# The meta tokens' state of gated linear attention in 128 rows, padded with zeros, instead of 16

## The chip, the cores and the metric

The kernel runs on one core of a Trainium2 chip. The metric is the device time of one execution in microseconds (us), lower is better. The core has five engines with a queue each: PE multiplies matrices (its weight loads have a row of their own in the profile, PEld), DVE and ACT work on vectors, POOL does small work and issues some transfers, and SP issues most of the transfers.

## The reference, cut to what matters

One decoder layer over 16 learned meta tokens followed by 512 tokens of width 1024. A retention branch and a gated linear attention branch (GLA) are computed from one input projection, gated, merged and projected. The GLA branch has four heads with keys of 128 and values of 256; its state decays by a gate of its own for every token and key channel:

```python
log_a = jax.nn.log_sigmoid((glr @ w_gate_up + b_gate)) / GLA_GATE_TAU
...
b = jnp.cumsum(ac, axis=2)
b_last = b[:, :, -1]
q_dec = qc * jnp.exp(b)
k_end = kc * jnp.exp(b_last[:, :, None] - b)
...
def step(state, xs):
    q_n, k_n, v_n, a_n = xs
    inter = jnp.einsum('bihd,bhde->bihe', q_n, state)
    state = state * jnp.exp(a_n)[..., None] + jnp.einsum('bjhd,bjhe->bhde', k_n, v_n)
    return state, inter
```

The meta tokens come first, so the state with which token 0 of the 512 starts is the sum over the 16 meta tokens of (key decayed to the end of the meta tokens) times value. Their outputs are dropped at the end.

## The kernel before, in words

Everything lies on 128 partitions ("rows" below). The 512 tokens are four blocks of 128; the meta tokens are a fifth, small block. Nearly all time goes to large projections by `quad` (a Strassen-like scheme of seven or so products; a product is 24 matmuls of line 327) and to branch products (lines 198 to 202). Every fp32 weight tile is split into a high and a low half by `split` (line 163: a copy on ACT, then a subtraction on DVE), so that each product is three matmuls of a faster type. Raw weights lie in six buffers (`wraw`), halves in three (`wsplit`); a load starts when a buffer is free.

Attention is woven in between: `weave` runs a generator of products and one of attention steps in turns. The planner of the program then gives each engine one fixed order by its own estimate of when things are ready, so instructions may stand elsewhere than the code has them. An engine works through its order without overtaking, apart from weight loads.

GLA is done for two pairs of heads, `gla_attention(0)` beside the products of `gla_g(0)`, and `gla_attention(1)` beside those of `gla_g(1)` (lines 1214 and 1217). Its steps, in the code's order (lines 1027 to 1057):

- `decays(b)`: splits the log gates `la` of block b into `lah` and `lal`, multiplies them on PE by 0/1 sums (`gsum`) into `ge` and `gf`, takes exponentials on ACT (`gX`), and makes four decayed copies of keys and queries on DVE (`gK`, `gQ`).
- `meta_state`: the same for the 16 meta tokens. Lines 976 and 977 multiply `lah` and `lal`, cut to 16 rows, by `gsm` (16 by 16); the exponential gives `gkm` (128 by 16), which is multiplied by the keys. `meta_state2` transposes it on PE (line 987, result in `gmt`) and copies it to `gkmt` on ACT (line 989), a tile of 16 rows; `meta_state3` multiplies it by the values `gvm`, also of 16 rows (line 995, a plain fp32 matmul, which the profile shows as two instructions), and DVE copies the result to `gS`, the first state (line 997).
- `scores(b)`: `gc` on PE (lines 957 to 961, the last a transpose), masked into `stb` by DVE (line 965).
- `values(b)`: lines 1006, 1007 and 1010 on PE: queries by state and scores by values into `go`, and the new state's addend `gsu`, which DVE adds (line 1012).

`gvm` is made once for each pair of heads, on ACT (lines 593 and 762). `gsm` comes from a constant through a small transfer and a cast on POOL (lines 739 to 742). Four `stb` tiles are set to zero on POOL (lines 1211 to 1213).

Of the kernel before, what the change touches and what calls it, by code (L numbers as in the profile page):

```python
# [21 lines left out]
F32 = mybir.dt.float32  # L22
F32R = mybir.dt.float32r
# [29 lines left out]
def constants():  # L53
    c = {}
    pos = np.concatenate([np.arange(NM, NM + 256), np.arange(HM),
                          np.arange(NM + 256, TT), np.arange(HM, NM)]).astype(np.float32)
    half = P
    inv = (10000.0 ** (-np.arange(half) / half)).astype(np.float32)
    ang = (pos[None, :] * inv[:, None].astype(np.float32)).astype(np.float32)
    c["rope"] = np.stack([np.cos(ang), np.sin(ang)], axis=1).astype(np.float32)  # L60

    j = np.arange(P)[:, None]
    cc = np.arange(T)[None, :]
    jm = np.arange(NM)[:, None]
    dec = np.zeros((4, P, 2, T), np.float64)
    for h in range(4):
        g = 1.0 - 2.0 ** (-5.0 - h)
        dec[h, :, 0] = np.where(cc >= j, g ** np.maximum(cc - j, 0).astype(np.float64), 0.0) / 16.0
        dm = g ** (NM + cc - jm).astype(np.float64) / 16.0
        for r in range(4):  # L70
            dec[h, 32 * r:32 * r + NM, 1] = dm
    c["decay"] = dec.astype(np.float32)

    m = np.arange(P)[:, None]
    i = np.arange(P)[None, :]
    U = (m <= i).astype(np.float64)
    mid = (np.arange(P) // 32) * 32 + 15
    Dm = U - U[:, mid]

    def level(w):  # L80
        s = (np.arange(P) // w) * w
        right = (np.arange(P) // w) % 2 == 1
        r = (m >= s[None, :]) & (m <= i)
        l = (m > i) & (m < (s + w)[None, :])
        return np.where(right[None, :], r, l).astype(np.float64)

    END = (m > i).astype(np.float64)
    c["gsum"] = (np.concatenate([U, Dm, level(64), level(32), END], axis=1) / 16.0).astype(np.float32)
    mm = np.arange(NM)
    c["gsum_meta"] = ((mm[:, None] > mm[None, :]) / 16.0).astype(np.float32)  # L90

    jj, ii = np.arange(P)[:, None], np.arange(P)[None, :]
    mA = (jj < 64) & (ii >= 64)
    mB = (jj // 64 == ii // 64) & (jj % 64 < 32) & (ii % 64 >= 32)
    mD = (jj // 32 == ii // 32) & (jj <= ii)
    c["gmask"] = np.stack([mA, mB, mD], axis=1).astype(np.int32)

    sel = np.zeros((P, P), np.float32)
    for g in range(4):
        for r in range(4):  # L100
            sel[32 * g + np.arange(NM), 32 * r + np.arange(NM)] = 1.0
    c["sel"] = sel
    oc = np.zeros((P, 1), np.float32)
    oc[[16, 48, 80]] = 1.0
    c["onecol"] = oc
    return c
# [3 lines left out]
def hybrid_kernel(ctx: ExitStack, tc: tile.TileContext, I, out: bass.AP):  # L110
# [51 lines left out]
    def split(hi, lo, src):  # L162
        return nc.scalar.copy(hi, src), nc.vector.tensor_sub(lo, src, hi.bitcast(F32))  # L163
# [10 lines left out]
    def act(ins):  # L174
        return queue("act", ins)
# [37 lines left out]
    def weave(dense, chain, skip=0):  # L213

        for n, _ in enumerate(dense):
            tick()
            if n >= skip:
                next(chain, None)
        for _ in chain:
            pass  # L220
# [298 lines left out]
    g1 = gctx.enter_context(tc.tile_pool(name="g1", bufs=1))  # L519
    la = g1.tile([P, 5, 512], F32, name="la")  # L520
    gsum = g1.tile([P, 640], F32R, name="gsum")
    gsm = g1.tile([NM, NM], F32R, name="gsm")
    gmask = g1.tile([P, 3, P], I32, name="gmask")
    gvm = [g1.tile([NM, 512], F32, tag="gvm", name=f"gvm{p}") for p in range(2)]
    gv = [g1.tile([P, NTB, 512], F32, tag="gv", name=f"gv{p}") for p in range(2)]
    gv0 = gv[0]

# [62 lines left out]

    def meta_v(psm, p):
        ps = meta_rows(psm, f"gvm{p}")
        nc.scalar.activation(gvm[p], ps[:NM], AF.Copy, scale=rt[:NM, NTB:])

    pss = [ppt(f"gv0_p{t}") for t in range(NTB)]
    casts = []
# [124 lines left out]
    for x in pmw:  # L721
# [14 lines left out]

    raws = (gsum[:, :512], xc.tile([P, 2, 256], F32, tag="xc", name="gs_raw").rearrange("p a b -> p (a b)"),
            I["gsum"][:, :512]), (gsum[:, 512:], laf[:, 2304:2432], I["gsum"][:, 512:]), \
        (gsm, fa[:NM, 1809:1809 + NM], I["gsum_meta"])
    for dst, raw, src in raws:  # L740
        nc.sync.dma_start(raw, src)
        nc.gpsimd.tensor_copy(dst, raw)
# [6 lines left out]
    def forget_gates():  # L749
# [9 lines left out]
                vec(nc.vector.scalar_tensor_tensor(g[32:64], pr[32:64, s, c0:c1], onec[32:64],  # L759
                                                   g[32:64].bitcast(F32), op0=ALU.add, op1=ALU.subtract))  # L760
        act(nc.scalar.copy(wzs, wz))
        act(nc.scalar.activation(gvm[0], gvs[:NM], AF.Copy, scale=rt[:NM, NTB:]))
        vec(nc.vector.tensor_sub(wzs[64:96], wz[64:96], wzs[64:96].bitcast(F32)))
        yield

# [87 lines left out]
                                     scale=(rt, rneg)[n][:, 2 * th + i:2 * th + i + 1])  # L853
        return f

    stb = []
    cnt = [0]
    G = {}

# [4 lines left out]
    def gla_g(p):  # L864
        sg = g1.tile([P, NTB, 512], F32, tag="gsg", name=f"gsg{p}")
        G["sg", p] = sg

        def evac(n, th, x, y):
            total(sg[:, 2 * th:2 * th + 2, n * 256:(n + 1) * 256], x, y)

        products = quad((C_GG + p * 512, C_GG + p * 512 + 256), True, f"gg{p}", evac, sooner=p == 0)
        if p == 0:
            yield from islice(products, 4)
            next(products)
            form(S4, u10, low)()
            yield
        yield from products
# [33 lines left out]
    def gla_attention(p):  # L911
# [3 lines left out]
        S = [None, None]  # L915
        Q, K, TO = {}, {}, {}

        def split_la(b, rows):
            if p == b == 0:
                return parts.pop("la")  # L920
            lh = gp.tile([P, 256], F32R, tag="lah", name=f"lah{p}{b}")
            ll = gp.tile([P, 256], F32R, tag="lal", name=f"lal{p}{b}")
            split(lh[:rows], ll[:rows], la[:rows, b, p * 256:(p + 1) * 256])
            return lh, ll

        def decays(b):
            lah, lal = split_la(b, P)
            for h in range(2):
                n = f"{p}{b}{h}"
                hc = h * P  # L930
                X = gp.tile([P, 6, P], F32, tag="gX", name=f"gX{n}", bufs=2)
                pe = pat(f"ge{n}")
                nc.tensor.matmul(pe[:, :256], lah[:, hc:hc + P], gsum[:, :256], start=True, stop=False)
                nc.tensor.matmul(pe[:, :256], lal[:, hc:hc + P], gsum[:, :256], start=False, stop=True)
                pf = pat(f"gf{n}")
                nc.tensor.matmul(pf[:, :384], lah[:, hc:hc + P], gsum[:, 256:], start=True, stop=False)
                nc.tensor.matmul(pf[:, :384], lal[:, hc:hc + P], gsum[:, 256:], start=False, stop=True)
                nc.scalar.activation(X[:, 0:2, :], pe[:, :256].rearrange("p (e t) -> p e t", e=2), AF.Exp)
                nc.scalar.activation(X[:, 5, :], pe[:, P:256], AF.Exp, scale=-1.0)
                G["exp"] = nc.scalar.activation(X[:, 2:5, :], pf[:, :384].rearrange("p (e t) -> p e t", e=3), AF.Exp)  # L940
                Q[b, h] = gp.tile([P, 4, P], F32, tag="gQ", name=f"gQ{n}", bufs=4)
                K[b, h] = gp.tile([P, 4, P], F32, tag="gK", name=f"gK{n}", bufs=2)
                TO[b, h] = sp.tile([P, 1], F32, tag="gto", name=f"gto{n}")
                qb = q[:, h, b * P:(b + 1) * P].unsqueeze(1).to_broadcast([P, 4, P])
                kb = k[:, h, b // 2, (b % 2) * P:(b % 2 + 1) * P].unsqueeze(1).to_broadcast([P, 4, P])
                nc.vector.tensor_mul(K[b, h], X[:, 2:6, :], kb)
                nc.vector.tensor_mul(Q[b, h], X[:, 0:4, :], qb)
                nc.gpsimd.tensor_copy(TO[b, h], X[:, 0, P - 1:P])
# [20 lines left out]
                    nc.scalar.copy(KT[b, h], pc[:, 3 * P:])  # L969

        def meta_state():
            lah, lal = split_la(4, NM)
            for h in range(2):
                hc = h * P
                pm = pat(f"gm{p}{h}")
                nc.tensor.matmul(pm[:, :NM], lah[:NM, hc:hc + P], gsm, start=True, stop=False)
                nc.tensor.matmul(pm[:, :NM], lal[:NM, hc:hc + P], gsm, start=False, stop=True)
                km = gp.tile([P, NM], F32, tag="gkm", name=f"gkm{p}{h}", bufs=2)
                nc.scalar.activation(km, pm[:, :NM], AF.Exp)
                km2 = km.rearrange("p (h m) -> p h m", h=2)  # L980
                nc.vector.tensor_mul(km2, km2, k[:, h, :, 256:HT])
                S[h] = km

        def meta_state2():
            for h in range(2):
                pt = pat(f"gmt{p}{h}")
                nc.tensor.transpose(pt[:NM, :P], S[h], ident)
                kmt = gp.tile([P, P], F32, tag="gkt", name=f"gkmt{p}{h}", bufs=3)[:NM]
                nc.scalar.copy(kmt, pt[:NM, :P])
                S[h] = kmt  # L990

        def meta_state3():
# [218 lines left out]
    for i in range(4):  # L1211
        stb.append(gp.tile([P, P], F32, name=f"stb{i}"))
        nc.gpsimd.memset(stb[i], 0.0)
    weave(gla_g(0), gla_attention(0), skip=1)
    weave(gla_qk(1), gla_output(0))
    drain(gla_v(1))
# [432 lines left out]
```

## Time and profile before

| what | value |
|---|---|
| median of 3 runs | 751.62 us (750.5 to 751.65) |
| the profiled execution, its own time | 750.33 us |
| its span in the profile | 748.6 us |
| ACT busy | 450.3 us (60%) |
| POOL busy | 137.5 us (18%) |
| mean transfer rate | 157 GB/s |

The span is what the profile covers; 1.73 us of the execution's own time lie outside it. Rows of the order of time read: start, duration, engine, line, operation, result<-operands, shape, count, and in brackets the engine's idle time before with what ended it. A matmul's shape is given as rows by columns of its weights, then rows by columns of what streams through. Matmul durations overlap (the next starts before the last has ended), so what one costs is read from the distance of starts. The meta tokens' instructions lie between 67 and 82 us (first pair of heads) and between 152 and 167 us (second pair).

### The profile page before, as it was taken

How to read it: one execution, taken by the hardware profiler on the slowest of the kernel's cores; microseconds unless marked ns; L12 is line 12 of the kernel's file. 1: busy time of each engine (PE TensorE's matmuls, PEld its weight loads, DVE VectorE, ACT ScalarE, POOL GpSimd, SP SyncE). 2: the span in 40 equal slices, each digit the busy share in tenths (PEclk: the TensorE clock that was granted, in tenths of full speed). 3: DMA queues.
4: the chain of work that ended last, by engine and by line, in shares of the span. 5: the costliest groups of instructions: out<-in, count | busy, mean ns of one | idle time of the engine just before them, and what ended most of it. 6: DMA issues, size and time to landing. Idle time of an engine off the chain costs nothing.

```text
span 748.6 us, 14064 instructions
## 1 busy us (share of the span) xinstructions
PE 738.6 (99%) x5595; PEld 691.7 (92%) x5595; DVE 607.7 (81%) x873; ACT 450.3 (60%) x764; POOL 137.5 (18%) x172
## 2 busy tenths in 40 slices
PE   9999999999999999999999999999999999999996
PEld 6799899989999999999989999989999989988996
DVE  6699877679897799888957688967697989775995
ACT  7898584666975466546546555646555656532562
POOL 2111110101221122110520100540011210111142
PEclk9999999999999999999999999999999999999999
DMA  9873521821589972734783652796476356687503
GB/s 298 278 162 77 121 62 53 198 85 58 129 187 280 305 169 87 170 113 141 200 250 115 133 149 96 199 213 163 126 169 136 113 141 197 227 195 206 133 29 113
DMA packets 100138, 117.42 MB, mean 157 GB/s; under 512 B 5732, under 2 KB 90852, under 8 KB 99816
## 3 DMA queue, kind: packets, MB, share of 16 engines
q1 hardware_dynamic: 79896, 88.19, 37.1%
q0 software_dynamic: 19888, 27.79, 20.4%
q8 instruction: 44, 0.72, 0.4%
q10 hardware_dynamic: 288, 0.53, 0.2%
q14 instruction: 22, 0.18, 0.1%
HBM read 104.44 MB, written 11.53 MB: 155 GB/s over the span
## 4 chain that ended last, share of the span: by engine, by line
PE 89%; DVE 7%; issue 2%; ACT 1%; POOL 0%; POOLq 0%; DVEq 0%; ACTq 0%
PE rqk_b L327 6%; PE rv_b L327 6%; PE rg_b L327 5%; PE rqk_c L327 5%; PE br_p L201 4%; PE br_p L202 4%; PE br_p L198 4%; PE gg_b L327 3%; PE mg_b L327 3%; PE mr_b L327 3%; PE gv_p L652 3%; PE rv_c L327 3%; PE bg_b L327 2%; PE rg_c L327 2%; PE gk_p L437 2%
## 5 line engine op out<-in xcount | busy, mean ns | idle before, releaser
L202 PE MATMUL br_p<-oh,br_l 128*128 128x512 f32 x128 | 49.9, 390 | 0.0
L201 PE MATMUL br_p<-ol,br_h 128*128 128x512 f32 x128 | 49.9, 390 | 0.0
L198 PE MATMUL br_p<-oh,br_h 128*128 128x512 f32 x128 | 49.8, 389 | 0.0
L163 ACT CAST rv_h<-rv_w 128x1024 fp32r<-128x1024 f32 x24 | 25.3, 1053 | 25.3 <-DVE rv_w L381 10.4
L327 PE MATMUL rqk_b<-xh,rqk_h 128*128 128x264 f32 (+1 forms) x128 | 36.2, 283 | 0.0
L327 PE MATMUL rqk_b<-xh,rqk_l 128*128 128x264 f32 (+1 forms) x128 | 36.1, 282 | 0.0
L327 PE MATMUL rqk_b<-xl,rqk_h 128*128 128x264 f32 (+1 forms) x128 | 36.0, 281 | 0.0
L327 PE MATMUL rv_b<-rv_l,xh 128*128 128x256 f32 x128 | 35.5, 277 | 0.5 <-DVE rv_l L163 0.5
L163 DVE TENSOR_TENSOR rv_l<-rv_w,rv_h 128x1024 fp32r<-128x1024 f32 x24 | 29.3, 1221 | 8.1 <-ACT rv_h L163 8.1
L327 PE MATMUL rv_b<-rv_h,xh 128*128 128x256 f32 x128 | 35.8, 280 | 0.0
L327 PE MATMUL rv_b<-rv_h,xl 128*128 128x256 f32 x128 | 35.4, 277 | 0.0
L327 PE MATMUL rg_b<-rg_h,xh 128*128 128x256 f32 x128 | 35.4, 277 | 0.0
L327 PE MATMUL rg_b<-rg_h,xl 128*128 128x256 f32 x128 | 35.4, 276 | 0.0
L327 PE MATMUL rg_b<-rg_l,xh 128*128 128x256 f32 x128 | 35.4, 276 | 0.0
L163 DVE TENSOR_TENSOR rg_l<-rg_w,rg_h 128x1024 fp32r<-128x1024 f32 x20 | 24.4, 1220 | 8.1 <-ACT rg_h L163 8.1
L163 ACT CAST rg_h<-rg_w 128x1024 fp32r<-128x1024 f32 x20 | 21.0, 1052 | 15.6 <-PE br_p L201 5.9
L291 POOL DMA_DIRECT2D rqk_x<-in_w_in_dram x8 | 10.4, 1302 | 102.2 <-PE rv_b L327 64.2
L202 PEld LDWEIGHTS br_p<-oh,br_l 128*128 128x128 f32 x128 | 24.0, 188 | 5.0
L1380 ACT ACTIVATE on<-av,nm,g_r 128x512 f32<-128x512 f32 x16 | 12.5, 779 | 26.4 <-DVE nm L1378 26.4
L198 PEld LDWEIGHTS br_p<-oh,br_h 128*128 128x128 f32 x128 | 24.0, 188 | 4.6
L201 PEld LDWEIGHTS br_p<-ol,br_h 128*128 128x128 f32 x128 | 24.0, 188 | 4.5
L163 ACT CAST rqk_h<-rqk_w 128x1024 fp32r<-128x1024 f32 x20 | 21.0, 1052 | 11.8 <-PE rqk_c L327 2.9
(624 smaller groups left out, 3155.4 us busy)
## 6 DMA issues: line engine op xcount, KB each, us to landing
rv_w<-in_w_in_dram SPq DMA_DIRECT2D x16, 512.0 KB, 4.2
br_w<-in_w_branch_ret_dram SPq DMA_DIRECT2D x16, 512.0 KB, 3.4
rqk_w<-in_w_in_dram SPq DMA_DIRECT2D x12, 512.0 KB, 5.0
rg_w<-in_w_in_dram SPq DMA_DIRECT2D x12, 512.0 KB, 4.9
rqk_x<-in_w_in_dram SPq DMA_DIRECT2D x8, 512.0 KB, 4.6
rqk_x<-in_w_in_dram POOLq DMA_DIRECT2D x8, 512.0 KB, 7.9
rg_x<-in_w_in_dram SPq DMA_DIRECT2D x8, 512.0 KB, 3.6
rg_x<-in_w_in_dram POOLq DMA_DIRECT2D x8, 512.0 KB, 7.6
```

The lines of the kernel that those rows point to most:

```text
L163: return nc.scalar.copy(hi, src), nc.vector.tensor_sub(lo, src, hi.bitcast(F32))
L198: m = nc.tensor.matmul(o, lh, rh, start=first, stop=False)
L201: nc.tensor.matmul(o, lh, rl, start=False, stop=False)
L202: m = nc.tensor.matmul(o, ll, rh, start=False, stop=last)
L291: x = nc.gpsimd.dma_start(t, block(0, 1), accum_op=ALU.add)
L327: m = nc.tensor.matmul(ps[t][:, :n] if wide else ps[t], l, r, start=first and j == 0, stop=kk == 3 and j == 2, skip_group_check=not fresh ...
L437: m = nc.tensor.matmul(pss[t][th], l[:, kk, c], r, start=first and j == 0, stop=kh == 1 and kk == 3 and j == 2, skip_group_check=not meta ...
L652: m = nc.tensor.matmul(pss[t], (al if j == 1 else ah)[t // 2, kh][:, k, c], (lo if j == 2 else hi)[:, kk, :], start=q == kk == j == 0, sto ...
L1380: nc.scalar.activation(on, ps, AF.Identity, scale=r, bias=nm)
```

## The change

Every operand of the meta tokens' state gets 128 rows. `gsm` is 128 by 16 with zeros below row 15. `lah` and `lal` are split in all 128 rows: what stands below row 15 is the finite gate of a zero input, and is multiplied by the zeros of `gsm`. The decayed keys are written to the first 16 columns of two lasting tiles `kms` (128 by 128), which POOL sets to zero once; the transpose takes all of a tile, so that `gkmt` has 128 rows with zeros below row 15. `gvm` has 128 rows, and its lower rows meet those zeros. The old tag `gkm` (two buffers of 16 columns) goes.

```diff
-    c["gsum_meta"] = ((mm[:, None] > mm[None, :]) / 16.0).astype(np.float32)
+    c["gsum_meta"] = np.concatenate([(mm[:, None] > mm[None, :]) / 16.0, np.zeros((P - NM, NM))]).astype(np.float32)
...
-    gsm = g1.tile([NM, NM], F32R, name="gsm")
+    gsm = g1.tile([P, NM], F32R, name="gsm")
...
-    gvm = [g1.tile([NM, 512], F32, tag="gvm", name=f"gvm{p}") for p in range(2)]
+    gvm = [g1.tile([P, 512], F32, tag="gvm", name=f"gvm{p}") for p in range(2)]
...
-        nc.scalar.activation(gvm[p], ps[:NM], AF.Copy, scale=rt[:NM, NTB:])
+        nc.scalar.activation(gvm[p], ps, AF.Copy, scale=rt[:, NTB:])
...
-        (gsm, fa[:NM, 1809:1809 + NM], I["gsum_meta"])
+        (gsm, fa[:, 1809:1809 + NM], I["gsum_meta"])
...
-        act(nc.scalar.activation(gvm[0], gvs[:NM], AF.Copy, scale=rt[:NM, NTB:]))
+        act(nc.scalar.activation(gvm[0], gvs, AF.Copy, scale=rt[:, NTB:]))
...
-            split(lh[:rows], ll[:rows], la[:rows, b, p * 256:(p + 1) * 256])
+            split(lh, ll, la[:, b, p * 256:(p + 1) * 256])
...
         def meta_state():
-            lah, lal = split_la(4, NM)
+            lah, lal = split_la(4)
             for h in range(2):
                 hc = h * P
                 pm = pat(f"gm{p}{h}")
-                nc.tensor.matmul(pm[:, :NM], lah[:NM, hc:hc + P], gsm, start=True, stop=False)
-                nc.tensor.matmul(pm[:, :NM], lal[:NM, hc:hc + P], gsm, start=False, stop=True)
-                km = gp.tile([P, NM], F32, tag="gkm", name=f"gkm{p}{h}", bufs=2)
-                nc.scalar.activation(km, pm[:, :NM], AF.Exp)
-                km2 = km.rearrange("p (h m) -> p h m", h=2)
+                nc.tensor.matmul(pm[:, :NM], lah[:, hc:hc + P], gsm, start=True, stop=False)
+                nc.tensor.matmul(pm[:, :NM], lal[:, hc:hc + P], gsm, start=False, stop=True)
+                nc.scalar.activation(kms[h][:, :NM], pm[:, :NM], AF.Exp)
+                km2 = kms[h][:, :NM].rearrange("p (h m) -> p h m", h=2)
                 nc.vector.tensor_mul(km2, km2, k[:, h, :, 256:HT])
-                S[h] = km
 
         def meta_state2():
             for h in range(2):
                 pt = pat(f"gmt{p}{h}")
-                nc.tensor.transpose(pt[:NM, :P], S[h], ident)
-                kmt = gp.tile([P, P], F32, tag="gkt", name=f"gkmt{p}{h}", bufs=3)[:NM]
-                nc.scalar.copy(kmt, pt[:NM, :P])
+                nc.tensor.transpose(pt[:, :P], kms[h], ident)
+                kmt = gp.tile([P, P], F32, tag="gkt", name=f"gkmt{p}{h}", bufs=3)
+                nc.scalar.copy(kmt, pt[:, :P])
                 S[h] = kmt
...
+    for h in range(2):
+        kms.append(gp.tile([P, P], F32, name=f"gkm{h}"))
+        nc.gpsimd.memset(kms[h], 0.0)
```

More of the change, by code (lines that the diff above doesn't have):

```diff
@@ L854, in rows_into @@
         return f
-    stb = []
+    stb, kms = [], []
     cnt = [0]
@@ L916, in gla_attention, with split_la @@
         Q, K, TO = {}, {}, {}
-        def split_la(b, rows):
+        def split_la(b):
             if p == b == 0:
@@ L922, in split_la @@
             ll = gp.tile([P, 256], F32R, tag="lal", name=f"lal{p}{b}")
-            split(lh[:rows], ll[:rows], la[:rows, b, p * 256:(p + 1) * 256])
+            split(lh, ll, la[:, b, p * 256:(p + 1) * 256])
             return lh, ll
         def decays(b):
-            lah, lal = split_la(b, P)
+            lah, lal = split_la(b)
             for h in range(2):
```

## The prediction

> **What bounds the kernel now.** I read the page first: the share of each engine, then the chain that ended last.
>
> ```profile
> span 748.6 us, 14064 instructions
> PE 738.6 (99%) x5595; PEld 691.7 (92%) x5595; DVE 607.7 (81%) x873; ACT 450.3 (60%) x764; POOL 137.5 (18%) x172
> PE 89%; DVE 7%; issue 2%; ACT 1%; POOL 0%; POOLq 0%; DVEq 0%; ACTq 0%
> ```
>
> PE is busy in 99% of the span and makes 89% of the chain, so PE time that goes is worth having. But DVE is at 81%, and 7% of the chain is its own: where DVE holds what PE needs next, a faster PE only waits. So I went on to the order of time on PE around the meta tokens' steps, and then to that on DVE, to see who is late next.
>
> The measure is the undisturbed distance of two dense matmuls, from a product in the chain in order of time:
>
> ```profile
> 129.22 2.72 PE gv_a L327 x24
> ```
>
> 2.72 / 24 = 0.113 us. Around line 976 of the first pair of heads, in PE's order of time:
>
> ```profile
> 67.57 0.28 PE L327 MATMUL gg_b<-gg_h,xl 128*128 128x256 f32 x1
> 67.77 0.38 PE L976 MATMUL gm<-gsm,lah 16*128 16x16 f32 x2
> 68.09 0.39 PE L327 MATMUL gg_c<-gg_h,xh 128*128 128x256 f32 x1
> 68.31 0.39 PE L957 MATMUL gc<-gQ,gK 128*128 128x128 f32 x2
> ```
>
> Around line 977 of the second pair:
>
> ```profile
> 155.24 0.28 PE L327 MATMUL gg_b<-gg_h,xh 128*128 128x256 f32 x1
> 155.45 0.38 PE L977 MATMUL gm<-gsm,lal 16*128 16x16 f32 x2
> 155.76 0.39 PE L327 MATMUL gg_b<-gg_l,xh 128*128 128x256 f32 x1
> 155.99 0.28 PE L327 MATMUL gg_b<-gg_h,xl 128*128 128x256 f32 x1
> ```
>
> And a short matmul in 128 rows, the transpose of line 961, with the next start:
>
> ```profile
> 69.49 0.27 PE L961 MATMUL gc<-ident,gK 128*128 128x128 f32 x1
> 69.60 0.39 PE L957 MATMUL gc<-gQ,gK 128*128 128x128 f32 x2
> ```
>
> From the dense matmul before to the second start behind (67.57 to 68.31) pass 0.74 us; two dense matmuls are 0.23 of it, so two tiny matmuls of 16 rows and 16 columns cost 0.51. At 155.24 it is 0.75, so 0.52. The reader should see where it goes: the start is late (0.20 instead of 0.11 behind the dense matmul), and the first dense matmul behind takes 0.22 instead of 0.11. Line 995, again in PE's order:
>
> ```profile
> 79.40 0.28 PE L327 MATMUL gg_c<-gg_l,xh 128*128 128x256 f32 x1
> 79.61 0.69 PE L995 MATMUL gs<-gvm,gkmt 16*128 16x256 f32 x2
> 80.23 0.38 PE L327 MATMUL gg_c<-gg_h,xl 128*128 128x256 f32 x1
> 80.45 0.28 PE L327 MATMUL gg_c<-gg_h,xh 128*128 128x256 f32 x1
> ```
>
> And line 1006, the same kind of matmul in 128 rows, with the next start:
>
> ```profile
> 82.20 0.59 PE L1006 MATMUL go<-gS,gQ 128*128 128x256 f32 x2
> 82.63 0.59 PE L1007 MATMUL go<-gv,stb 128*128 128x256 f32 x2
> ```
>
> 79.40 to 80.45 is 1.05; less two dense matmuls 0.82. Line 1006 does the same two passes over 256 columns in 128 rows in 82.63 - 82.20 = 0.43, with no delay in front. So 16 rows cost 0.39 us more than 128.
>
> **The change part by part.**
>
> *Lines 976 and 977*: four groups of two, each 0.515 now. In 128 rows they stream 16 columns, which no row shows; bounds are 0 and the present 0.515 for a group. The nearest row is line 961 (128 rows, 128-column weights, a short stream): 69.49 to 69.60, 0.11 each, so 0.22 for a group. I take that: 4 x 0.295 = 1.18 saved.
>
> *Line 995*: four heads at 0.39: 1.56 saved.
>
> *Line 987*, the transpose, gets 128 columns of weights instead of 16:
>
> ```profile
> 72.89 0.28 PE L327 MATMUL gg_c<-gg_h,xl 128*128 128x256 f32 x1
> 73.01 0.38 PE L987 MATMUL gmt<-ident,gkm 128*16 128x128 f32 x2
> 73.14 0.36 PE L327 MATMUL gg_b<-gg_h,xh 128*128 128x256 f32 x1
> 73.35 0.28 PE L327 MATMUL gg_b<-gg_l,xh 128*128 128x256 f32 x1
> ```
>
> 72.89 to 73.35 is 0.46, less 0.23: 0.117 for each of two; line 961 with full weights takes 0.11. I take no difference. The Trainium skill speaks against the change here (TensorE: Matmul & The Clock Gate, "LDWEIGHTS (loading the stationary operand)"): a weight load takes its columns divided by 1.2, in ns, whatever the rows. By that page's figures 112 more columns would be an estimated 0.09 us for each transpose, 0.37 us for four, and the PE sum below would be 2.37; the rows just shown do not have it.
>
> PE saves 1.18 + 1.56 = 2.74 us by rows. Beside PE:
>
> ```profile
> L762 ACT ACTIVATE gvm<-gvm_s,rt 16x512 f32<-16x512 f32 x1 | 0.7, 676 | 0.0
> L781 ACT ACTIVATE gv<-gv,rt 128x512 f32<-128x512 f32 x4 | 2.6, 708 | 0.0
> L1213 POOL MEMSET stb<- x4: 198/198/198, 3.9 to 4.3; 128x128 f32 x4
> L588 POOL CAST sel<-la x1: 345/345/345, 17.9 to 17.9; 128x128 fp32r<-128x128 f32 x1
> ```
>
> The same activation takes 676 ns in 16 rows and 708 in 128, so splits, copies and `gvm` cost ACT and DVE nothing worth counting. Two more memsets of 128 by 128 are 0.4 us on POOL; the four like them run at 3.9 to 4.3 us, and POOL's cast behind them comes at 17.9, so they are hidden. Without that gap they would delay POOL by 0.4 us once. The constant's transfer on SP's queue grows from 1 to 8 KB; `gsm` is first read at 67.77, far behind it.
>
> *Who is late next.* Line 995 needs `gkmt`, and line 1006 the state `gS`. ACT in order of time:
>
> ```profile
> 79.04 0.25 ACT L989 COPY gkmt<-gmt 16x128 f32<-16x128 f32 x1
> ```
>
> DVE in order of time:
>
> ```profile
> 70.58 1.09 DVE L965 COPY_PREDICATED stb<-gmask,gc 128x128 f32<-128x128 int32 x5 [0.47 <-PE gc L961]
> ...
> 80.85 0.74 DVE L997 COPY gS<-gs 128x256 f32<-128x256 f32 x2
> ```
>
> First pair: the second head's `gkmt` is there at 79.29. PE could start its line 995 at 79.51 and wants it 0.39 earlier, 79.12; so it waits 0.17. PE's gain at line 1006 is 2 x 0.295 + 2 x 0.39 - 0.17 = 1.20: from 82.20 to 81.00. The first state is there at 80.85 + 0.41 = 81.26 (half of the copy of two) and DVE closes its gap of 0.47 behind PE: 80.79. It fits: 1.20 passes; had DVE not moved, 0.94.
>
> Second pair, DVE again:
>
> ```profile
> 151.70 0.69 DVE L946 TENSOR_TENSOR gK<-gX,gk 128x512 f32<-128x512 f32 x1 [1.81 <-ACT gX L940]
> ...
> 159.21 1.22 DVE L163 TENSOR_TENSOR gg_l<-gg_w,gg_h 128x1024 fp32r<-128x1024 f32 x1
> 162.33 1.23 DVE L364 TENSOR_TENSOR mr_x<-mr_w,mr_w 128x1024 f32<-128x1024 f32 x1 [1.90 <-DMA mr_w<-in_w_in_dram]
> ...
> 165.88 0.42 DVE L997 COPY gS<-gs 128x256 f32<-128x256 f32 x1
> ```
>
> And PE's line 1006 of this pair, and the transfers of `mr_w` on SP's queue:
>
> ```profile
> 166.78 0.59 PE L1006 MATMUL go<-gS,gQ 128*128 128x256 f32 x2
> L297 SPq DMA_DIRECT2D mr_w<-in_w_in_dram x4: 367/368/368, 142.5 to 158.0; - x4
> ```
>
> DVE works without a gap from 151.70, ahead of the first 16-row matmul there, to 160.4. Then it stands 1.90 us at line 364 for a weight load, the last of four, issued at 158.0 when DVE has freed its buffer. Nothing in that depends on what PE saves behind 152; so the copy of the first state stays at 165.88 and ends at 166.30. Line 1006 begins at 166.78: PE can gain 0.48 and then waits, though by its rows it would have gained 1.37 less such waits as the first pair's. I take 0.48.
>
> Sum: 1.20 + 0.48 = 1.68 us. Against the profiled execution's 750.33 us (span 748.6 and 1.73 around it) that is 748.65. The median of the runs shown is 751.62, 1.29 above the profiled execution; from it the forecast is 749.94, say **749.9**. That later stretches pass it on rests on the page: PE leads the chain and its loads are released by what runs.
>
> **The rivals.**
>
> *All of PE's saving arrives.* Speaks for it: the planner makes a new order, and a `mr_x` that stands behind the state copies would free line 1006. Against: the widths by which it plans hardly change. 2.74 gives 748.9; with padded matmuls at no cost (4 x 0.515 + 1.56 = 3.62) 748.0.
>
> *Less passes on.* DVE has hardly a gap from 162 on, so a wait of PE behind DVE further down may take the first pair's gain too. What is left is the second pair's 0.48, or 751.1. For it: DVE's 7% of the chain. Against: where the chain goes over DVE it comes back to PE.
>
> *Rows don't matter.* The delay may come from the short stream or the change of data type. Then nothing is saved: 751.6. The Trainium skill has a rule for it (TensorE: Matmul & The Clock Gate, "Why this matters for your kernels"): a single matmul of 32 rows takes as long as one of 128, and only several side by side gain. Line 995 against line 1006 speaks against it: the same type and stream, 0.82 and 0.43. Another page of the Trainium skill, TensorEngine Tiling (Array Packing), "Key Properties", says that changing the tiling mode drains the array; by that rule the late starts (0.20 for 0.11) are such drains, and the trace agrees. If only lines 976 and 977 save nothing, the first pair gives 0.61 (2 x 0.39 - 0.17) and the second 0.48: 750.5, within the forecast's range.
>
> *Slower: line 1006 moves forward.* The planner puts the first `values` step of both pairs ahead of a product that now stands in front, because it counts the state as ready sooner. The state is not (80.79 and 166.30), so PE stands idle: a product is 2.72 us. First pair: 2.72 less the 0.21 between 80.79 and 81.00, second 2.72; less 1.68 it is 3.55 slower: 755.2. It decides from 17 matmuls moved ((1.68 + 0.21) / 0.113), both pairs together. Against: the shapes that set its estimates stay nearly as they were.
>
> **How the numbers follow.** Forecast (savings 1.0 to 2.3, so 749.3 to 750.6) 0.50; all arrives 0.15; less passes on 0.17; rows don't matter 0.08; slower 0.10. A measurement of this kernel tells about 0.2%, 1.5 us, from no change: the three runs spread over 1.15. Faster by more than that: three fifths of the forecast and a little, 0.33, and 0.15, 0.48. Slower: 0.10. Within: the rest, 0.42. The range 747.9 to 752.2 takes in all cases but the slower one, down to padded matmuls at no cost and up to no gain with half of the runs' spread.
>
> **What would show it.** The 16-row forms are gone; lines 976 and 977 in 128 rows take about 0.22 for two, line 995 0.43; dense matmuls behind them are 0.11 apart. PE shows a new wait of about 0.6 us for `gS` ahead of line 1006 near 165, and one of 0.17 at line 995. The span from 84 to 148 is 1.2 earlier, from 167 on 1.7. If line 1006 of the second pair begins 2.5 or more earlier without waiting, the limit by DVE was wrong; if the groups still cost 0.5, the rows were. The forecast also fails if the two lasting tiles, which shift the addresses of those behind, make later work wait for them, or if the planner's order differs elsewhere.

## The result, and the profile after

The changed kernel takes 749.08 us, the median of 8 runs (748.4 to 749.76); the kernel before took 751.0 beside it, also 8 runs (749.9 to 751.65). The ratio is 0.9973, with a 95% interval of 0.9963 to 0.9982, so 1.9 us less, between 1.4 and 2.8. The forecast was 749.9, 1.7 us less: the saving is near it, while the time itself lies 0.8 below it, because the forecast started from the median of three runs of the kernel before, 751.62, where eight runs give 751.0. The profiled execution of the changed kernel took 748.97 us, 1.36 less than that of before. The head of its page and its chain by engine:

```profile
span 747.2 us, 14066 instructions
PE 736.7 (99%) x5595; PEld 691.7 (93%) x5595; DVE 606.9 (81%) x873; ACT 450.2 (60%) x764; POOL 138.8 (19%) x174
...
PE 83%; DVE 9%; ACT 3%; DMA 2%; issue 2%; POOL 1%; POOLq 0%; DVEq 0%; ACTq 0%; SPq 0%
```

PE has the same 5595 matmuls and 1.9 us less of busy time. But its part of the chain fell from 89% to 83%: DVE, ACT and a transfer took it over, the first sign that another step is late now. Line numbers behind the change have moved by two: the meta tokens' product is line 993 now, the copy of its state 995, `values` 1004 to 1008.

Line 976 of the first pair, in PE's order of time:

```profile
67.30 0.28 PE L327 MATMUL gg_b<-gg_h,xl 128*128 128x256 f32 x1
67.42 0.28 PE L976 MATMUL gm<-gsm,lah 128*128 128x16 f32 x2
67.56 0.36 PE L327 MATMUL gg_c<-gg_h,xh 128*128 128x256 f32 x1
67.76 0.38 PE L957 MATMUL gc<-gQ,gK 128*128 128x128 f32 x2
```

From 67.30 to 67.76 is 0.46 us, less two dense matmuls (0.23): 0.23 for the two, where it was 0.51. The start is 0.12 behind the dense matmul ahead, no longer 0.20. Line 993, both heads of the first pair:

```profile
77.37 0.63 PE L993 MATMUL gs<-gvm,gkmt 128*128 128x256 f32 x2
77.65 0.47 PE L327 MATMUL gg_c<-gg_l,xh 128*128 128x256 f32 x1
77.96 0.28 PE L327 MATMUL gg_c<-gg_h,xl 128*128 128x256 f32 x1
...
78.19 0.28 PE L327 MATMUL gg_c<-gg_l,xh 128*128 128x256 f32 x1
78.36 0.70 PE L993 MATMUL gs<-gvm,gkmt 128*128 128x256 f32 x2
78.70 0.47 PE L327 MATMUL gg_c<-gg_h,xl 128*128 128x256 f32 x1
79.01 0.28 PE L327 MATMUL gg_c<-gg_h,xh 128*128 128x256 f32 x1
```

PE's second head starts right behind the end (78.31) of ACT's copy that it needs:

```profile
78.04 0.27 ACT L987 COPY gkmt<-gmt 128x128 f32<-128x128 f32 x1
```

First head: 77.37 to 77.96 is 0.59, less one dense matmul 0.48. Second head: 78.19 to 79.01 is 0.82, less two, 0.59. Before, the second head cost 0.82.

The second pair, PE around its first `values` step, then DVE's order and one of PE's waits:

```profile
164.29 0.28 PE L327 MATMUL gg_b<-gg_h,xl 128*128 128x256 f32 x1
164.90 0.70 PE L1004 MATMUL go<-gS,gQ 128*128 128x256 f32 x2 [0.34 <-DVE gS L995]
```

```profile
160.88 1.23 DVE L364 TENSOR_TENSOR mr_x<-mr_w,mr_w 128x1024 f32<-128x1024 f32 x1 [2.11 <-DMA mr_w<-in_w_in_dram]
...
164.43 0.75 DVE L995 COPY gS<-gs 128x256 f32<-128x256 f32 x2
```

```profile
PE bg_b L327 <- DVE gs L1150: 0.2, 1, 0.2
```

The waits at lines 1004 and 1150 are new. DVE stands 2.11 us for the load where it stood 1.90, and the state is copied behind it. The idle time of 0.34 is counted from the end of the matmul ahead; by starts, 164.29 to 164.90, PE lost 0.50.

**Where the time went** is read best as a lead: how much earlier an instruction starts than the same one in the trace of before. Each execution also begins a little earlier or later, ahead of anything that the change touches, so the table takes off the lead that a run had at 60 us. Places are times of the trace of before.

| kernel | median us, ratio to before | lead at 84 | at 166.8 | at 236 | at 292 | at the end |
|---|---|---|---|---|---|---|
| changed | 749.08, 0.9973 | 1.15 | 1.56 | 1.07 | 1.06 | 1.03 |
| changed, once more | 749.65, 0.9978 | 1.20 | 1.69 | 1.58 | 0.64 | 0.65 |
| sums alone | 750.3, 0.9996 | 0.53 | 0.88 | 0.59 | 0.58 | 0.52 |
| states alone | 749.83, 0.9983 | 0.58 | 1.15 | 0.94 | 0.93 | 0.92 |
| state copy on ACT | 749.1, 0.9975 | 1.15 | 2.06 | 0.70 | 0.14 | 0.09 |
| add behind the copy | 749.16, 0.9972 | 1.15 | 2.02 | 1.12 | 0.96 | 0.91 |
| line 728 too | 749.54, 0.9980 | 1.16 | 1.25 | 0.30 | 0.18 | 0.13 |
| accumulating transfer first | 749.07, 0.9973 | 1.15 | 1.47 | 1.28 | 0.96 | 0.94 |
| that and the add | 748.69, 0.9966 | 1.13 | 2.01 | 1.82 | 1.81 | 1.78 |
| those and line 728 | 747.98, 0.9959 | 1.13 | 2.01 | 1.82 | 1.81 | 1.78 |

The first two rows agree with the forecast at 84 (1.20) and at 166.8 (1.68). Behind that a part is lost, in one execution ahead of 236, in the other ahead of 292.

### The profile page after: what moved, and what is told of

Read it like the earlier page. It is cut to its first block, busy times and chain, and to the rows that moved or that the text cites. A ratio compares the mean times of both kernels' runs of the same rounds, so it can differ in the third digit from the quotient of the medians.

```text
span 747.2 us, 14066 instructions
## 1 busy us (share of the span) xinstructions
PE 736.7 (99%) x5595; PEld 691.7 (93%) x5595; DVE 606.9 (81%) x873; ACT 450.2 (60%) x764; POOL 138.8 (19%) x174
## 4 chain that ended last, share of the span: by engine, by line
PE 83%; DVE 9%; ACT 3%; DMA 2%; issue 2%; POOL 1%; POOLq 0%; DVEq 0%; ACTq 0%; SPq 0%
PE rqk_b L327 6%; PE rv_b L327 6%; PE rg_b L327 5%; PE rqk_c L327 5%; PE br_p L201 4%; PE br_p L202 4%; PE br_p L198 4%; PE mg_b L327 3%; PE gv_p L652 3%; PE rv_c L327 3%; PE gg_b L327 2%; PE rg_c L327 2%; PE bg_b L327 2%; PE mr_b L327 2%; PE gk_p L437 2%
```

## The experiments

**Each half of the change alone.** The first kernel pads lines 976 and 977 only, the second all but these; diffs here and below are against the changed kernel, cut to their core:

```diff
-    gvm = [g1.tile([P, 512], F32, tag="gvm", name=f"gvm{p}") for p in range(2)]
+    gvm = [g1.tile([NM, 512], F32, tag="gvm", name=f"gvm{p}") for p in range(2)]
...
-                nc.tensor.transpose(pt[:, :P], kms[h], ident)
+                nc.tensor.transpose(pt[:NM, :P], S[h], ident)
```

```diff
-    gsm = g1.tile([P, NM], F32R, name="gsm")
+    gsm = g1.tile([NM, NM], F32R, name="gsm")
...
-                nc.tensor.matmul(pm[:, :NM], lah[:, hc:hc + P], gsm, start=True, stop=False)
+                nc.tensor.matmul(pm[:, :NM], lah[:NM, hc:hc + P], gsm, start=True, stop=False)
```

> The change's part at lines 976 and 977 alone: gsm, lah and lal in 128 rows; the transpose, gkmt, gvm and line 995 as before, in 16 rows. Theory (16 rows delay PE; in the second pair PE then waits for the state gS): two matmuls of lines 976 and 977 cost 0.22 to 0.23 us instead of 0.51, line 995 still 0.82; the first pair gains 0.58, the second 0.45 to 0.48, 1.05 in all against before. Rival, rows don't matter: the groups stay at 0.5 and the time is that of before. Rival, no limit by DVE: 1.18.

> The rest of the change alone: kms, gkmt and gvm in 128 rows, so line 995 in 128 rows; gsm, lah and lal in 16 rows as before. Theory: line 995 costs 0.43 to 0.49 instead of 0.82, the groups of lines 976 and 977 stay at 0.51; the first pair gains 0.61 (0.78 less the wait for gkmt), the second 0.48 and then waits for gS, 1.09 in all against before. Together with the run of the sums alone that is 2.1, more than the whole change has (1.68), because the second pair's limit is met twice. Rival, no limit by DVE: 1.56 here, and the two parts add up to the whole. Rival, rows don't matter: nothing.

Sums alone: 750.3 us, ratio 0.9996 (0.9987 to 1.0005). States alone: 749.83, ratio 0.9983 (0.9974 to 0.9992). In the traces the terms come apart cleanly. With the sums alone a group of two takes 0.23 and the second head's product, still of 16 rows, 0.83; with the states alone it is 0.52 and, for the first head's product, 0.47. At 84 the leads 0.53 and 0.58 add up to 1.11, near the whole's 1.15 and 1.20. At 166.8 they add up to 0.88 + 1.15 = 2.03, more than the whole's 1.56 and 1.69. In neither half does the profile show a wait for the state in the second pair; only together do they meet a limit there. Between 84 and 166.8 the sums alone gained 0.35, less than the 0.45 to 0.48 that was expected; the reason stands below, under "The rows".

**Is the limit DVE's copy of the state?** Two ways to take it away: ACT makes the copy for the second pair, or DVE's add that waits for the load (line 364) is ordered behind the copies.

```diff
-                nc.vector.tensor_copy(s0, ps[:, :256])
+                (nc.scalar.copy if p else nc.vector.tensor_copy)(s0, ps[:, :256])
```

```diff
-            nc.vector.tensor_add(x3, w22, w12)
+            (lambda m: name == "mr0" and after(m, G["s0"]))(nc.vector.tensor_add(x3, w22, w12))
...
-                nc.vector.tensor_copy(s0, ps[:, :256])
+                G["s0"] = nc.vector.tensor_copy(s0, ps[:, :256])
```

> The changed kernel with one more edit: in the second pair of heads the copy of the first state to gS is made on ACT instead of DVE, so that it doesn't stand behind line 364, which waits for a weight load. Theory (that wait is the limit): the first line 1004 of the second pair (1006 of before) starts without the wait of 0.34 us and about 0.6 earlier against line 977 than in the changed kernel; 0.4 to 0.6 us less in the whole time, if nothing takes it up until 235 us. Rival, another wait stands right behind (the queries gQ of the pair, or the weights): the start moves by under 0.2 and the time stays.

> The changed kernel with DVE's line 364 for mr_x ordered behind the copies of the second pair's first states (line 995), instead of ahead of them. It undoes the limit that the forecast named in another way than the copy on ACT does, and leaves the copy on DVE. Theory: DVE makes gK, gQ and the copies while the load of mr_w is under way, the first line 1004 of the second pair starts without the wait of 0.34 us, 0.5 to 0.6 earlier counted from line 977, and the lead over the kernel before is 2.3 to 2.4 at 167 us. The time: 0.4 to 0.6 less than the changed kernel's if the accumulating transfer at 224 lets it pass, else the same time with a longer wait at 226. Rival, mr_x is late now for its own use and takes it back at 185 to 200.

With ACT: 749.1 us, ratio 0.9975 (0.9966 to 0.9984). With the add later: 749.16, ratio 0.9972 (0.9961 to 0.9984). Neither differs from the changed kernel. The rows of the second (DVE, then PE):

```profile
163.55 0.75 DVE L995 COPY gS<-gs 128x256 f32<-128x256 f32 x2
...
168.50 1.22 DVE L364 TENSOR_TENSOR mr_x<-mr_w,mr_w 128x1024 f32<-128x1024 f32 x1
```

```profile
164.73 0.59 PE L1004 MATMUL go<-gS,gQ 128*128 128x256 f32 x2
```

The wait at line 1004 is gone, and the lead there is 2.06 and 2.02: that was the limit. (The second was expected at 2.3 to 2.4; what it lacks stands below, under "The rows".) It does not reach the end. Both kernels show a longer wait further down, here in the one with the add later:

```profile
PE bg_b L327 <- DVE gs L1150: 0.7, 1, 0.7
```

By 236 the leads are 0.70 and 1.12. In both, and in the last two kernels below, the planner also moved some twenty neighbouring instructions, so their later parts are not the changed kernel's to the letter.

**Is it the few rows, and does a gain further up arrive?** Line 728 has the same form, two tiny matmuls of 16 rows, at 33 us, and was untouched by the change. Its operands lie in 128 rows already:

```diff
-    m = nc.tensor.matmul(rbp[:, HT:HT + NM], ones[:NM], dg[:NM, NTB, :NM], start=False, stop=True, skip_group_check=True)
+    m = nc.tensor.matmul(rbp[:, HT:HT + NM], ones, dg[:, NTB, :NM], start=False, stop=True, skip_group_check=True)
```

> The changed kernel with the last 16-row matmul, line 728 at 33.5 us, in 128 rows too (the rows below 15 of its second operand are zeros already). Theory (any 16-row group between 128-row matmuls pays): from the last start of line 726 to the second start of line 437 behind it 1.02 us become 0.75 to 0.8, and PE is 0.25 earlier at 58 us. Rival: the delay there hangs on the data or the place, and the distance stays at 1.02. Whether the end moves is open: under the noise of the time in any case.

749.54 us, ratio 0.998 (0.9971 to 0.9989). PE's order of this kernel, and then of the kernel before:

```profile
32.45 1.02 PE L726 MATMUL rb<-la 128*128 128x512 f32 x2
33.31 0.29 PE L728 MATMUL glr<-la 128*128 128x16 f32 x2
...
33.65 0.28 PE L437 MATMUL gq_p<-xl,gq_h 128*128 128x256 f32 x1
```

```profile
32.56 1.02 PE L726 MATMUL rb<-la 128*128 128x512 f32 x2
33.51 0.39 PE L728 MATMUL glr<-la 16*128 16x16 f32 x2
...
34.05 0.28 PE L437 MATMUL gq_p<-xl,gq_h 128*128 128x256 f32 x1
```

From line 726 to the last start pass 1.20 instead of 1.49: 0.29 gained by rows alone, in other code and with other data. (It lies ahead of 60 us, so the table leaves it out.) But PE then waits 0.7 for `gS` at line 1004 in the one execution profiled, against 0.34 in the changed kernel, and 0.7 again at line 1150. DVE stood 2.43 us for the load there instead of 2.11, and its copy of the state began at 164.65 instead of 164.43. So the gain met the same limit, and a later load besides. The median shows no gain over the changed kernel.

**How many rows does it take?** The same kernel with 64 and with 96 rows in lines 976, 977 and 993 (all that is left out holds zeros). One execution each.

```diff
-    gsm = g1.tile([P, NM], F32R, name="gsm")
+    gsm = g1.tile([64, NM], F32R, name="gsm")
...
-                nc.tensor.matmul(ps[:, :256], S[h], vm[:, h * 256:(h + 1) * 256], start=True, stop=True)
+                nc.tensor.matmul(ps[:, :256], S[h][:64], vm[:64, h * 256:(h + 1) * 256], start=True, stop=True)
```

> Where the delay of 16 rows begins: the changed kernel with lines 976, 977 and 993 cut to the first 64 of the 128 rows (the rest of the rows are zeros). Theory (anything under the full height of the array makes PE wait for what runs and hold up what follows): the groups of lines 976 and 977 are back at 0.5 us, line 993 at 0.82, as with 16 rows. Rival, the delay belongs to very low matmuls only: 0.23 and 0.48 as in the changed kernel. Second rival, it grows as rows get fewer: about half the delay, 0.35 and 0.65.

> The same with 96 rows. Theory: 96 rows don't fit in half of the height, so they count as full: 0.23 for a group of lines 976 and 977, 0.48 for line 993. Rival, every matmul under 128 rows pays: 0.5 and 0.82.

PE's order with 64 rows, then with 96:

```profile
68.18 0.28 PE L327 MATMUL gg_b<-gg_h,xl 128*128 128x256 f32 x1
68.38 0.39 PE L976 MATMUL gm<-gsm,lah 64*128 64x16 f32 x2
...
80.01 0.28 PE L327 MATMUL gg_c<-gg_l,xh 128*128 128x256 f32 x1
80.22 0.70 PE L993 MATMUL gs<-gvm,gkmt 64*128 64x256 f32 x2
...
81.06 0.28 PE L327 MATMUL gg_c<-gg_h,xh 128*128 128x256 f32 x1
```

```profile
67.23 0.28 PE L327 MATMUL gg_b<-gg_h,xl 128*128 128x256 f32 x1
67.34 0.29 PE L976 MATMUL gm<-gsm,lah 96*128 96x16 f32 x2
...
78.12 0.28 PE L327 MATMUL gg_c<-gg_l,xh 128*128 128x256 f32 x1
78.28 0.70 PE L993 MATMUL gs<-gvm,gkmt 96*128 96x256 f32 x2
...
78.94 0.28 PE L327 MATMUL gg_c<-gg_h,xh 128*128 128x256 f32 x1
```

With 64 rows the second head's product takes 81.06 - 80.01 less 0.23, 0.82, exactly what 16 rows took, and the start of line 976 is late by the same 0.20. With 96 rows it takes 0.59 and 0.11, what 128 rows take. The delay is a step, not a price for each missing row. The Trainium skill (TensorEngine Tiling (Array Packing), "Tiling Modes") lists arrangements of the array in tiles of 128, 64 and 32 rows, none of 96; "Key Properties" there says that changing the mode drains the array. Both agree with the step lying between 64 and 96, and with a delay on either side of the small matmul; no run shows the mode itself. The single times, 752.35 and 748.57 us, lie as these rows have them, but one run each proves nothing of the total.

**Is the wait at line 1150 the accumulating transfer?** Line 1150 takes the low half of a weight form from `og`, behind a transfer that adds one `og` tile to another (line 1139). First the transfer was replaced by POOL's own addition:

```diff
-        nc.gpsimd.dma_start(a00, a01, accum_op=ALU.add)
+        nc.gpsimd.tensor_add(a00, a00, a01)
```

> The changed kernel with the sum of line 1139 (og plus og1gq, 128 by 1024) made by an addition on POOL instead of an accumulating transfer that takes 9.0 us to land and is what the last of the seven forms of the GLA branch (lines 1149 and 1150) waits for. Theory (that wait took 0.37 us of the gain at 232 us): POOL has the sum some 2 to 3 us after 215, line 1149 doesn't wait, the last product of the first GLA branch starts without its 0.16 us wait, and the lead over the kernel before that stands at 1.76 us at 220 stands there at 285 too; 0.4 us less in the time. Rival, DVE itself is late there (it works without a gap from 209 to 225), so line 1150 comes no earlier, or POOL's addition slows DVE: the lead falls to 1.4 all the same, or lower.

751.84 us, ratio 1.001 (1.0002 to 1.0019): all of the change's gain was given back. POOL's and DVE's rows at that place, and PE's longest wait:

```profile
215.25 2.90 POOL L1139 TENSOR_TENSOR og<-og,og1gq 128x1024 f32<-128x1024 f32 x1
```

```profile
215.30 3.94 DVE L163 TENSOR_TENSOR bg_l<-bg_w,bg_h 128x1024 fp32r<-128x1024 f32 x1
```

```profile
PE bg_a L327 <- DVE bg_l L163: 2.2, 1, 2.2
```

POOL's addition took 2.90 us, from 215.25 to 218.15. The DVE subtraction that began beside it took 3.94 instead of 1.22, and PE waited 2.2. The rival, that POOL's addition slows DVE, fits this trace, and the run says nothing against the transfer as the cause.

Then its place in POOL's queue. Transfers of POOL, ACT's first use of the result, and the transfer as the chain of the changed kernel has it:

```profile
214.15 1.33 POOL L291 DMA_DIRECT2D bg_x<-in_w_branch_gla_dram  x1 [1.38 <-DMA bg_x<-in_w_branch_gla_dram]
214.96 1.45 POOL L1139 DMA_DIRECT2D og<-og1gq  x1
...
224.16 1.06 ACT L1149 ACTIVATE gs<-og 128x1024 fp32r<-128x1024 f32 x1 [1.18 <-DMA og<-og1gq]
```

```profile
214.96 9.02 DMA og<-og1gq
```

A weight transfer of the next product group stands directly ahead, which does not need to. In the next kernel it stands behind:

```diff
-        nc.gpsimd.dma_start(a00, a01, accum_op=ALU.add)
+        G["acc"] = nc.gpsimd.dma_start(a00, a01, accum_op=ALU.add)
...
-                            forms=[[gforms[i][x] for i in range(7)] for x in range(2)], early=True)
+                            forms=[[gforms[i][x] for i in range(7)] for x in range(2)], early=True, behind=G["acc"] if j else None)
```

Line 292 lets `behind` hold back this group's `x3`, too. The changed kernel itself was run again beside it, and so was this edit with the later add, and with both and line 728:

> The changed kernel once more, for times beside the three runs after it and for a second trace. Theory: the lead over the kernel before is 1.2 us at 84, 1.7 at 167 (counted from the start of line 976 in the first pair), some 0.4 less from 233 on, depending on how late the accumulating transfer lands (9.0 us in the first trace); the time 1 to 2 us below before.

> The changed kernel with POOL's two accumulating transfers near 214 us in the other order: og (line 1139) first, then the weight load bg_x of the second GLA product group, which is needed only after 235 us. Orders on all other engines stay. Theory (og lands 9 us after its issue because 512 KB of bg_x lie in front of it in the same queue): og lands 4 to 6 us after its issue, by 220; line 1149 doesn't wait for it, PE has no wait at 226.5, and the lead of 1.7 at 220 stands at 285: 0.4 to 0.7 less in the time than the changed kernel. Rival, the transfer is slow by itself or by the other loads: it lands after 8 us or more, at 222 to 223, which is 1 us less late and lets most of the gain pass anyway; second rival, bg_x is late for its product near 236 and takes the gain back.

> Both limits taken away: og first on POOL, and DVE's line 364 behind the copies of the second pair's states. Theory: the lead is 2.0 to 2.3 at 167 and, if nothing else is near, 2 at 285 and in the time, 0.5 to 1 less than the changed kernel. Rival, DVE from 200 to 225 is a limit of its own with little slack: the lead falls back to 1.4 to 1.7 by 233.

> The same with line 728 in 128 rows too. Theory: 0.25 more lead from 34 us on, all of it at 285: 2.2 to 2.5 us below before at the end, the fastest of the kernels here. Rival: the extra 0.25 goes into a wait, and the time is that of the run before.

The changed kernel again: 749.65 us, ratio 0.9978 (0.997 to 0.9987). The transfer first: 749.07, ratio 0.9973 (0.9963 to 0.9983). With the later add: 748.69, ratio 0.9966 (0.9954 to 0.9978). With line 728: 747.98, ratio 0.9959 (0.9946 to 0.9971), the fastest kernel of the study, 3.5 us under the kernel before (751.45) and 1.7 under the changed one, all run together. The two intervals still touch, but each of its five runs (747.69 to 748.72) is below all eleven of the changed kernel (748.87 to 750.1). With the transfer first, the rows of POOL and ACT, and the time from issue to landing:

```profile
215.69 0.92 POOL L1139 DMA_DIRECT2D og<-og1gq  x1 [1.98 <-DVE gs L163]
216.31 1.65 POOL L291 DMA_DIRECT2D bg_x<-in_w_branch_gla_dram  x1
...
223.82 1.06 ACT L1149 ACTIVATE gs<-og 128x1024 fp32r<-128x1024 f32 x1
```

```profile
DMA to landing us min/median/max: 5.6/5.6/5.6
```

ACT waits no more. The transfer of `og` lands 5.6 us after its issue here, 6.4 with the later add, against 9.0 and 8.5 in the two traces of the changed kernel and 8.2 in that of before. Alone this does little (there is little left to wait for). Its lead falls from 1.28 to 0.96 behind 236, but not by a wait, as the second rival had it: from 237.5 to 244.5 the same matmuls of line 327 start 0.118 apart instead of 0.113, and why is not shown. With the add it keeps 1.78 of 2.01 us to the end, and in those two kernels PE holds 91% of the chain and DVE 6%. By medians the pair's step over the changed kernel is about 1 us, and the last step, line 728's, 0.7 where its rows give 0.29; both are inside the intervals. So the times show the three edits together, and only the traces separate the steps.

What the changed kernel loses further down, its second trace shows elsewhere, in the waits of PE:

```profile
PE rg_c L327 <- DVE rg_l L163: 1.2, 2, 0.6
```

In the first trace that line is 0.6 in one wait, as in the trace of before. So the same program lost 0.49 ahead of 236 and nothing further down in one execution, and 0.94 between 236 and 292 in the other.

The wait at line 1150 does not need a gain to arise. The kernel with 64 rows, whose small matmuls are as slow as those of before, is 0.15 behind the trace of before at 220. It then waits longer there than any other, and is 1.40 behind at 236:

```profile
PE bg_b L327 <- DVE gs L1150: 0.9, 1, 0.9
```

## Why the prediction was right, step by step

**The rows.** Right for three of the four groups of lines 976 and 977, and for line 995. The forecast for a group of two was 0.22, and 0.23 was measured; for line 995 (now 993) 0.43, and 0.48 was measured on the first head. Line 728 and the run with 96 rows confirm that rows do it, and not the short stream or the data type, as the rival "rows don't matter" had it: only the rows differ there. One sign that was named did not come: the dense matmuls behind are not 0.11 apart at once, but 0.20 behind line 976 (67.56 to 67.76) and 0.31 behind line 993.

The remaining group, line 976 of the second pair, saved almost nothing. Before, and then after:

```profile
152.33 0.39 ACT L163 CAST lah<-la 16x256 fp32r<-16x256 f32 x1
152.77 0.38 PE L976 MATMUL gm<-gsm,lah 16*128 16x16 f32 x2
```

```profile
150.87 0.45 ACT L163 CAST lah<-la 128x256 fp32r<-128x256 f32 x1
151.37 0.39 PE L976 MATMUL gm<-gsm,lah 128*128 128x16 f32 x2
```

In both, PE starts 0.05 behind the end of ACT's split of `lah`, and the start is late by this wait. The group cost 0.66 before (152.42, the dense matmul ahead, to 153.31, less 0.23) and 0.62 after (150.96 to 151.81). The prediction counted 0.515 and 0.22 here, and nothing for the split, which takes 0.06 longer in 128 rows. By its terms PE would have led by 2.40 just ahead of line 1004 (1.20 for each pair); the first trace has 2.05. The forecast of the time did not suffer, because line 1004 waits for the state anyway.

**The wait of the second head.** Right: the start follows ACT's copy by 0.05 (78.31, 78.36). Forecast 0.17, measured about 0.11 (0.59 less the first head's 0.48). Product and wait together were forecast at 0.60 and took 0.59.

**The transposes.** Forecast as no difference. Their order of time after:

```profile
72.05 0.28 PE L327 MATMUL gg_c<-gg_h,xl 128*128 128x256 f32 x1
72.16 0.38 PE L985 MATMUL gmt<-ident,gkm 128*128 128x128 f32 x2
...
72.50 0.28 PE L327 MATMUL gg_b<-gg_l,xh 128*128 128x256 f32 x1
```

0.45 with 128 columns of weights, 0.46 with 16. The weight load itself is longer, 0.140 us on PEld instead of 0.089, but PE's starts do not show it. The Trainium skill's price by columns (TensorE: Matmul & The Clock Gate, "LDWEIGHTS (loading the stationary operand)") would have made it 0.64 by the estimate in the prediction; the measurement decides.

**First pair, 1.20.** The lead at 84 is 1.15 and 1.20 in two traces.

**Second pair, 0.48.** The lead grows from 84 to 166.8 by 0.41 and 0.49. That DVE's copy behind the load is the limit was shown: with the copy on ACT, or the add moved behind it, the sum at 166.8 is 2.06 and 2.02. The wait was forecast at 0.6, and shows as 0.34 and 0.27 of idle time, 0.50 by starts in the first trace. "All of PE's saving arrives" falls with that; not even the 2.05 ahead of line 1004 did.

**"That later stretches pass it on"** was the weak step; only a part is passed on, as the rival "less passes on" said. Of 1.56 and 1.69 at 166.8 the traces keep 1.03 and 0.65. One loss lies where ACT and DVE wait for the accumulating transfer, the other at DVE's halves for `rg`. The prediction had looked for DVE alone and had no row of the transfer.

Yet the medians differ by 1.9 and 1.8 us, more than these leads. The trace of before is one execution, of 750.33 us, 0.7 quicker than its median beside the changed kernel. If other executions of before lose something further down too, the differences fit. The kernel with 64 rows, which loses 1.25 between 220 and 236 without any gain, makes that likely; for the kernel before itself it was not shown, and how large the kept part is remains open. That 1.9 came out so near to 1.7 is therefore in part luck: the sum at 166.8 was right for the reasons given, and the way from there to the end was not. The order of the planner did not turn against the change: the slower rival did not come, and no product was moved ahead of the state.

## What to carry to other kernels

In this kernel a lone matmul of 16 or 64 rows in a stream of 128-row matmuls costs more than the same matmul in 128 rows, 0.28 us for a pair of tiny ones and 0.35 for an fp32 one of 256 columns, unless it waits for its operand anyway; where zeros can be had without further work, pad it. Then look for what is late next, and do not add up the parts: 2.0 us of halves gave 1.6 at the first limit. A limit taken away alone (here DVE's wait for a load) could not be told from none; that, the place of a transfer in its queue and one more padded pair gave 1.7 us together.

## What was not expected of the hardware

- 64 rows cost what 16 cost (0.82 us), and 96 what 128 cost (0.59 with the wait).
- The dense matmul that follows the first one behind line 993 in 128 rows comes 0.31 us after it, not 0.11 (77.65 to 77.96); but 77.65 is only 0.03 behind the start of line 993's second pass (77.62), so most of that pass lies in the 0.31. What makes the product 0.48 and not 0.43 is in its first pass: 0.25 (77.37 to 77.62), where each pass of line 1004 takes 0.22.
- In one trace a POOL addition of two tiles of 128 by 1024 took 2.90 us, and the DVE subtraction that began 0.05 behind it took 3.94 instead of 1.22.
- The accumulating transfer of 512 KB landed 5.6 to 6.4 us after its issue when it stood ahead of another accumulating transfer in POOL's queue (three traces), and 8.2 to 9.2 behind it (ten traces).
